# Two-layer hybrid gMLP and attention trunk: last gate tile's statistics deferred in layer 0, keys turned later, gated products' low parts moved to VectorE in layer 1

## The chip, the cores and the metric

The kernel runs on 1 core of one Trainium2 chip. The metric is the device time of one execution in microseconds; lower is better. Times below are medians of several executions, except where a profiled execution is named.

## What is computed

Two layers over 512 latent and 256 context tokens of width 1024, all in float32. In each layer one input projection gives queries (8 heads), keys and values (2 heads), and two 512-wide halves `u` and `g` of a gated mixer. The mixer normalises `gelu(g)` in groups of 128 channels, mixes it over 128 positions with a small matrix, and multiplies by `gelu(u)`:

```python
def chunk_gmlp(u, vg, w_s, b_s, g_norm):
    u = gelu(u)
    vg = group_layernorm(gelu(vg).reshape(b, n, 4, 128), g_norm)   # mean, variance of each group
    mixed = einsum('gpq,bnqgc->bnpgc', w_s, vg_by_chunks_of_128) + b_s
    return u * mixed
# one layer
attn = gqa(rope(rmsnorm(q)) * 64 ** -0.5, rope(rmsnorm(k)), v)     # context attends context, latents all
x = x + ga1 * (concat([attn, chunk_gmlp(u, g)]) @ w_out)
x = x + ga2 * (square(relu(modulate(rmsnorm(x), sh2, sc2) @ w_ff1)) @ w_ff2)
```

`sh`, `sc`, `ga` come from a modulation product of two condition vectors with `w_mod` (1024 x 6144 in each layer). In the last layer only the latents go past the keys and values.

## The kernel before, in words

**Numbers in two parts.** A float32 operand is split into a high part, rounded to the multiplier's format (`hi`, a cast by ScalarE), and the rest (`lo`, a subtraction by VectorE or GpSimd; `split`, L221 and L222). A product is three matmuls: high by high, high by low, low by high. Weights arrive as `raw` (two buffers), are split into a ring of five `hi`/`lo` pairs, and go back to the ring after their last use. The weights of layer 0's output projection are split by GpSimd (`PAR["WP"]`), the modulation weights of the later chunks are loaded straight into ring pairs and used in plain float32 (`mod_chunk`, L354).

**Order.** The program is written once, and a scheduler in the tile framework fixes each engine's order before the run. The author steers it with a virtual clock (`Flow`): each matmul advances it, and `fl.defer(delay, f)` has `f` written so much later. In the run every engine works through its own fixed list, one after the other.

**Layer 0, projections (about 55 to 168 us).** `sink_kv` and `sink_q` take the keys and queries of a pair of 128-token tiles (`tp` = 0, 1, 2; 2 is the context): norm and rotation (`qk`), then a split into a stack `k` (`stack`, one buffer, L722 to L725), then eight TensorE transposes and two copies (`turn`, L735, L736), `late(tp)` after the projection. After them come the `u` tiles and the gate tiles (`sink_g`, two column halves by three tile pairs). For a gate tile VectorE does the two steps of GELU (L802, L806), the statistics of four groups (L854, L855), a reciprocal square root of ten small instructions (L857, L301 to L311), and the normalisation (L860); ScalarE and GpSimd split the result (L221, L222); 13.6 us of virtual time later comes the mixing: twelve small matmuls into PSUM (`pt<-ws,e` and `pt<-ws,acc`, L217), scale and bias by VectorE (L884), product with `u` by GpSimd (L889).

**Layer 0, attention (from about 168 us).** Four context tiles of 128 queries of a head come first (`attn_tile`): scores into `pa`, maximum by VectorE (L982), exponential by ScalarE (L985), transposes by TensorE (L1001), split of the transposed weights (L1003, L1004), product with the values. Between them stand products that fill: modulation chunks (L354, with a transpose by VectorE, L362, and four small matmuls, L367) and the output projection of the gated products. `make_gm` prepares these products: it writes all mixings still due, then splits the four `U` tiles (L931 casts, L932 subtractions; the first two on VectorE, the other two on GpSimd).

**Layer 1** has the same stages with 512 tokens. GpSimd does its square roots (L298), the sums and products of the rotation (L707, L717), and the splits of the output weights. Its `make_gm` stands behind the last query tile, in front of attention, with low parts again two on VectorE and two on GpSimd.

PSUM holds two buffers each of `a` (scores, `u` tiles), `b` (projections, values, modulation) and `t` (transposes, mixings, small products): a product that needs a buffer waits until the last reader of the product two before it is done.

Of the kernel before, what the change touches and what calls it, by code (L numbers as in the profile page):

```python
# [8 lines left out]
F32 = mybir.dt.float32  # L9
F32R = mybir.dt.float32r  # L10
# [161 lines left out]
def trunk(ctx: ExitStack, tc: tile.TileContext, xT, pk1, pk2, rope, wsT, w_mod, w_tok, w_u, w_out, w_ff1, w_ff2, outT):  # L172
# [16 lines left out]
    def unit(tag, shape, dt=F32R):  # L189
        return units.tile(shape, dt, tag=tag, name=nm(tag))  # L190
# [10 lines left out]
    def te(dt=F32):  # L201
        return tmp.tile([128, 512], dt, tag="e", name=nm("e"), bufs=3)

    def small(n, dt=F32, tag="m", bufs=9):
        return tmp.tile([128, n], dt, tag=tag, name=nm(tag), bufs=bufs)
# [88 lines left out]
    def rsqrt(v, n, l=0):  # L294

        if l:
            y = small(n)
            pool_e.tensor_tensor(out=y, in0=v, in1=mhalf[:, 0:n], op=ALU.pow)  # L298
            return y
        yi = small(n, I32)  # L300
        vec.tensor_scalar(yi, v.bitcast(I32), -0.5, 1595932665.0, op0=ALU.mult, op1=ALU.add)  # L301
        y = yi.bitcast(F32)
        t, r = small(n), small(n)
        vec.tensor_tensor(out=t, in0=y, in1=y, op=ALU.mult)
        vec.scalar_tensor_tensor(out=t, in0=t, scalar=-0.703952253, in1=v, op0=ALU.mult, op1=ALU.mult)
        vec.scalar_tensor_tensor(out=y, in0=t, scalar=1.681914091, in1=y, op0=ALU.add, op1=ALU.mult)
        vec.tensor_tensor(out=t, in0=y, in1=y, op=ALU.mult)
        vec.tensor_tensor(out=r, in0=t, in1=v, op=ALU.mult)
        vec.tensor_scalar(t, r, 0.375, -1.25, op0=ALU.mult, op1=ALU.add)
        vec.tensor_tensor(out=t, in0=t, in1=r, op=ALU.mult)  # L310
        vec.scalar_tensor_tensor(out=y, in0=t, scalar=1.875, in1=y, op0=ALU.add, op1=ALU.mult)  # L311
        return y
# [364 lines left out]
    def layer(l, h, nxt, K, kv=None, kv0=0):  # L677
# [76 lines left out]
            fl.defer(PAR["QK%d" % l] if wait is None else wait, one)  # L754

        def late(tp):
            return 13000.0 + 8000.0 * tp if tp < 2 else 18000.0

        def sink_kv(tp, ps, pool=False):
            heads = lambda a: a.rearrange("p (h d) -> p h d", d=64)  # L760
# [11 lines left out]
                vec.tensor_tensor(out=vd[:, :, :, 64:128], in0=vps, in1=vd[:, :, :, 0:64].bitcast(F32), op=ALU.subtract)  # L772
            turned(t1, 2, 1, tp, [(kA, [(0, 0), (1, 0)]), (kB, [(0, 64), (1, 64)])], late(tp) if pool else None)

        def sink_q(grp):
            def f(tp, ps, pool=False):
                if tp == 0:
                    for f_ in mixes if grp and l else ():
                        f_()
                    Q.extend(unit(f"B{3 + grp * 2 + i}", [128, 2, T]) for i in range(2))  # L780
                ps = [p.rearrange("p (h d) -> p h d", d=64) for p in ps] if isinstance(ps, list) else ps.rearrange("p t (h d) -> p t h d", d=64)
                t1 = qk(ps, tp, 4, 0, pool)
                turned(t1, 4, 0, tp, [(Q[grp * 2 + i], [(2 * i, 0), (2 * i + 1, 0)]) for i in range(2)], late(tp) + 4000.0 if pool else None)
            return f
# [63 lines left out]
        def sink_g(gp):  # L848
            def f(tp, ps):
                v = gelu2(None, ps.rearrange("p t n -> p (t n)"), [128, 512])  # L850
                st = small(24, tag="bn", bufs=2).rearrange("p (a b) -> p a b", b=6)
                mv = small(8, tag="mv", bufs=2).rearrange("p (a b) -> p a b", b=2)
                for i in range(4):
                    vec.bn_stats(out=st[:, i, :], in_=v[:, i * 128:i * 128 + 128])  # L854
                    vec.bn_aggr(out=mv[:, i, :], in_=st[:, i, :])  # L855
                ve = small(4)
                vec.tensor_scalar(ve, mv[:, :, 1], 4 * EPS, None, op0=ALU.add)  # L857
                r = rsqrt(ve, 4, l)
                for i in range(4):
                    (pool_e if l in PAR['VG'] else vec).tensor_scalar(v[:, i * 128:i * 128 + 128], v[:, i * 128:i * 128 + 128], mv[:, i, 0:1], r[:, i:i + 1], op0=ALU.subtract, op1=ALU.mult)  # L860
                if len(mixes) > 1:
                    mixes[-2]()
                if l:
                    vg = unit(("B5", "B6")[len(mixes) % 2], [128, 2, 512])
                    vg = [vg[:, 0, :], vg[:, 1, :]]
                else:
                    vg = [te(F32R), tmp.tile([128, 512], F32R, tag="acc0", name=nm("acc0"), bufs=1) if len(mixes) % 2 else te(F32R)]
                split(*vg, v, pool_e if l in PAR['VL'] else vec)

                @once  # L870
                def mixing():
                    mx = pt((128, 2, 256))
                    for g in range(2):
                        for t in range(2):
                            c = slice(t * 256 + g * 128, t * 256 + g * 128 + 128)
                            w = slice((gp * 2 + g) * 128, (gp * 2 + g) * 128 + 128)
                            for i, (a, b) in enumerate(((0, 0), (0, 1), (1, 0))):
                                mm(mx[:, g, t * 128:t * 128 + 128], vg[a][:, c], ws[:, b, w], i == 0, i == 2, 128)
                    u = U[gp][:, :, tp * 256:tp * 256 + 256]
                    e = tsm([128, 2, 256])  # L880
                    for g in range(2):
                        G_ = gp * 2 + g
                        to = u if G_ == LATE[l] else e
                        vec.scalar_tensor_tensor(out=to[:, g, :].rearrange("p (t q) -> p t q", t=2), in0=mx[:, g, :].rearrange("p (t q) -> p t q", t=2),  # L884
                                                 scalar=gnh[:, G_:G_ + 1], in1=P2("bs")[:, G_ * 128:G_ * 128 + 128].unsqueeze(1).broadcast_to([128, 2, 128]),
                                                 op0=ALU.mult, op1=ALU.add)
                    gs = [g for g in range(2) if gp * 2 + g != LATE[l]]
                    gs = slice(gs[0], gs[-1] + 1)
                    pool_e.tensor_tensor(out=u[:, gs], in0=e[:, gs], in1=u[:, gs], op=ALU.mult)  # L889
                mixes.append(mixing)  # L890
                fl.defer(PAR["G%d" % l], mixing)
            return f

        with region('proj%d' % l):
# [22 lines left out]
        with region('q%d' % l):  # L917
            for g in range(2) if l else ():
                qp = TokProj(l, 1 + g, h, NP, sink_q(g))
                for tp in range(NP):  # L920
                    qp.bank(tp)

        GM = []

        def make_gm():
            for f in mixes:
                f()
            for g in range(4):
                gm = unit(f"A{g}", [128, 2, T])
                src = U[g // 2][:, g % 2, 0:TQ]  # L930
                act.copy(gm[:, 0, 0:TQ], src)  # L931
                (pool_e if g > 1 else vec).tensor_tensor(out=gm[:, 1, 0:TQ], in0=src, in1=gm[:, 0, 0:TQ].bitcast(F32), op=ALU.subtract)  # L932
                GM.append(gm)


        def gate(i, m, off, n, src):
            for a, b, cond in ((0, SEQ, 0), (SEQ, T, 1)):
# [113 lines left out]
                                fl.fill0(goal)  # L1051

        def gm_out():
            make_gm()
            yield from proj4(("out", l, 0), GM, 2, [dense], "b")

        def mods(js):
# [262 lines left out]
```

## Time and profile before

| | |
|---|---|
| median of 3 runs | 1504.56 us (1504.34 to 1506.78) |
| the profiled execution, its own time | 1504.58 us |
| its span, first to last instruction | 1502.8 us |
| TensorE busy | 1452.6 us (97%) |
| mean granted TensorE clock | 0.993 |
| TensorE busy in 100 to 200 us | 88.50 of 100 us |
| TensorE busy in 1000 to 1100 us | 97.24 of 100 us |

The profile shows for each instruction when it began and how long it took, and puts idle time of an engine down to the one that released it. A line of the chain or of the timeline gives start, duration, engine, source line, operation, output from inputs. "Idle before" stands in square brackets with the releaser behind the arrow. PE is TensorE, DVE VectorE, ACT ScalarE, POOL GpSimd, SP the queue that issues loads.

### The profile page before, as it was taken

What the parts mean: (1) busy time and instruction counts of PE and PEld (TensorE: products, weight loads), DVE (VectorE), ACT (ScalarE), POOL (GpSimd) and SP (SyncE); (2) the same over time, 40 slices, a digit from 0 to 9 for tenths busy, and PEclk for the clock granted to TensorE, in tenths of its full rate; (3) what the DMA queues carried; (4) which work ended last, traced back from release to release, by engine and by line L of the source; (5) the groups of instructions that cost most, each with busy time, mean ns of one, the idle gap of its engine ahead of it and who ended that gap; (6) DMA issues with size and microseconds to landing.
All of it is one profiled execution on the core that took longest, in us unless ns stands there. A gap on an engine that the chain in (4) does not pass through costs nothing.

```text
span 1502.8 us, 21987 instructions
## 1 busy us (share of the span) xinstructions
PE 1452.6 (97%) x8626; PEld 1276.0 (85%) x8626; DVE 893.1 (59%) x1603; ACT 638.0 (42%) x1081; POOL 359.9 (24%) x335
## 2 busy tenths in 40 slices
PE   6999799999999999999999999999999999999998
PEld 3889677798889899898989889897889888888887
DVE  5838867787755555444444536766887544444443
ACT  3542345665545453433333324536774333322221
POOL 0332331312045552322323213256122000000000
PEclk9999899999999999999999999999999999999999
DMA  9312524201134334333333311221001323333221
GB/s 365 106 57 86 181 89 171 94 15 43 61 111 129 116 120 127 104 122 112 127 113 126 99 56 52 90 85 57 29 1 57 113 98 98 98 99 98 99 97 58
DMA packets 50088, 148.78 MB, mean 99 GB/s; under 512 B 5440, under 2 KB 6976, under 8 KB 49984
## 3 DMA queue, kind: packets, MB, share of 16 engines
q1 hardware_dynamic: 49408, 146.72, 29.4%
q8 instruction: 68, 1.11, 0.3%
q10 hardware_dynamic: 576, 0.66, 0.1%
q14 instruction: 36, 0.29, 0.1%
HBM read 145.26 MB, written 2.10 MB: 98 GB/s over the span
## 4 chain that ended last, share of the span: by engine, by line
PE 83%; DVE 8%; ACT 3%; POOL 3%; issue 2%; DMA 1%; SPq 0%; POOLq 0%; ACTq 0%; DVEq 0%
PE pa L217 54%; PE pb L217 21%; PE pt L1001 3%; PE pt L217 2%; PE pb L354 2%; POOL m L298 1%; ACT hi L221 1%; DVE lo L222 1%; DMA A<-in_w_mod 1%; DVE X L941 1%; PE pt L735 1%; DVE B L1121 1%; POOL lo L222 1%; DVE s L860 0%; ACT w L985 0%
## 5 line engine op out<-in xcount | busy, mean ns | idle before, releaser
L217 PE MATMUL pa<-A,hi 128*128 128x384 f32 (+2 forms) x1728 | 458.6, 348 | 1.8 <-ACT w L1114 1.0
L221 ACT CAST hi<-raw 128x1024 fp32r<-128x1024 f32 x168 | 176.5, 1051 | 467.4 <-PE pa L217 386.0
L222 DVE TENSOR_TENSOR lo<-raw,hi 128x1024 fp32r<-128x1024 f32 x152 | 193.2, 1271 | 238.6 <-ACT hi L221 235.0
L217 PEld LDWEIGHTS pa<-A,hi 128*128 128x128 f32 x1728 | 310.8, 188 | 26.0 <-ACT w L1114 2.7
L217 PE MATMUL pa<-A,lo 128*128 128x384 f32 (+2 forms) x864 | 299.3, 347 | 0.0
L217 PE MATMUL pa<-B,hi 128*128 128x512 f32 (+1 forms) x900 | 239.8, 355 | 3.6 <-DVE X L941 3.6
L403 POOL TENSOR_TENSOR C<-C,s 128x512 f32<-128x512 f32 x112 | 164.4, 1483 | 315.8 <-ACT s L402 273.9
L217 PEld LDWEIGHTS pa<-B,hi 128*128 128x128 f32 x900 | 158.7, 188 | 31.7 <-DVE X L941 5.9
L217 PEld LDWEIGHTS pa<-A,lo 128*128 128x128 f32 x864 | 162.8, 189 | 10.6
L941 DVE SCALAR_TENSOR_TENSOR X<-pa,modT,X 128x512 f32<-128x512 f32 x126 | 82.9, 660 | 141.8 <-PE pa L217 141.8
L217 PE MATMUL pb<-B,hi 128*128 128x512 f32 (+1 forms) x600 | 156.7, 349 | 2.0 <-DVE X L941 2.0
L217 PE MATMUL pa<-B,lo 128*128 128x512 f32 (+1 forms) x450 | 157.7, 354 | 0.0
L941 DVE SCALAR_TENSOR_TENSOR X<-pb,modT,X 128x512 f32<-128x512 f32 (+3 forms) x116 | 70.9, 619 | 83.9 <-PE pb L217 83.6
L217 PE MATMUL pb<-hi,A 128*128 128x256 f32 (+1 forms) x608 | 118.3, 291 | 0.5 <-DVE m L715 0.5
L217 PEld LDWEIGHTS pb<-B,hi 128*128 128x128 f32 x600 | 104.2, 189 | 16.5 <-DVE X L941 3.2
L217 PE MATMUL pb<-B,lo 128*128 128x512 f32 (+1 forms) x300 | 104.6, 349 | 0.0
L217 PEld LDWEIGHTS pb<-hi,A 128*128 128x128 f32 x608 | 97.0, 191 | 2.2 <-PE pb L217 0.7
L217 PEld LDWEIGHTS pa<-B,lo 128*128 128x128 f32 x450 | 84.0, 188 | 11.3
L402 ACT ACTIVATE s<-k,silu 128x512 f32<-128x512 f32 x112 | 77.0, 716 | 38.4 <-DMA k<-in_w_mod 29.0
L217 PE MATMUL pb<-lo,A 128*128 128x256 f32 (+1 forms) x304 | 87.7, 288 | 0.0
L985 ACT ACTIVATE w<-pa,m 128x768 f32<-128x768 f32 (+1 forms) x80 | 65.6, 820 | 35.2 <-DVE m L982 33.4
L1004 DVE TENSOR_TENSOR A<-pt,A 128x384 fp32r<-128x384 f32 (+1 forms) x144 | 73.3, 536 | 11.1 <-ACT A L1003 9.3
(196 smaller groups left out, 2203.3 us busy)
## 6 DMA issues: line engine op xcount, KB each, us to landing
raw<-in_w_ff SPq DMA_DIRECT2D x128, 512.0 KB, 3.5
k<-in_w_mod SPq DMA_DIRECT2D x96, 256.0 KB, 3.1
raw<-in_w_tok SPq DMA_DIRECT2D x16, 512.0 KB, 3.5
raw<-in_w_out SPq DMA_DIRECT2D x16, 512.0 KB, 3.5
lo<-in_w_mod SPq DMA_DIRECT2D x16, 512.0 KB, 4.5
hi<-in_w_mod SPq DMA_DIRECT2D x16, 512.0 KB, 4.2
A<-in_w_mod SPq DMA_DIRECT2D x8, 512.0 KB, 9.9
B<-in_w_mod SPq DMA_DIRECT2D x8, 512.0 KB, 9.7
```

The costliest lines, as they stand in the source:

```text
L217: pe.matmul(out, a, b, start=start, stop=stop)
L221: act.copy(hi, src)
L222: (eng or vec).tensor_tensor(out=lo, in0=src, in1=hi.bitcast(F32), op=ALU.subtract)
L298: pool_e.tensor_tensor(out=y, in0=v, in1=mhalf[:, 0:n], op=ALU.pow)
L354: pe.matmul(ps[q:q + 32, :], S32[:, k, :], ws_[k2 // 2][:, k2 % 2 * 512:(k2 % 2 + 1) * 512], start=k < ns, stop=k >= KT - ns)
L402: act.activation(p, w, AF.Copy, scale=s)
L403: pool_e.tensor_tensor(out=a, in0=a, in1=p, op=ALU.add)
L735: pe.transpose(p[:, o:o + 128], stk[:, t, hh, c0:c0 + 128].bitcast(F32), ident)
L941: vec.scalar_tensor_tensor(out=xs, in0=src[:, s - off:e - off], scalar=modT[l][:, i * 8 + m, cond:cond + 1], in1=xs, op0=ALU.mult, op1=ALU ...
L985: act.activation(p, ps[:, 0:nk], AF.Exp, bias=nmx, accum_out=sm)
L1001: pe.transpose(tp_[:, (kt - k0) * 128:(kt - k0) * 128 + 128], p[:, kt * 128:kt * 128 + 128], ident)
L1004: vec.tensor_tensor(out=ptl[:, k0:k0 + step, d], in0=src, in1=pth[:, k0:k0 + step, d].bitcast(F32), op=ALU.subtract)
```

## The change

Three edits. First, in `sink_g` everything behind GELU (statistics, square root, normalisation, split) becomes a function `rest`; for the last gate tile of layer 0 (`n == 2 * NP - 1`) it is deferred by 8.0 us of virtual time, and its mixing by 21.6 instead of 13.6; all others run it at once as before. Second, `late` gives longer delays to tile pairs 1 and 2. Third, `make_gm` moves up in the code, is called in layer 1 from the last query tile's `sink_q` ahead of its norm, and has all four low parts on VectorE in layer 1.

```diff
         def late(tp):
-            return 13000.0 + 8000.0 * tp if tp < 2 else 18000.0
+            return 13000.0 + 11000.0 * tp if tp < 2 else 22000.0
...
+        def make_gm():
+            for f in mixes:
+                f()
+            for g in range(4):
...
+                act.copy(gm[:, 0, 0:TQ], src)
+                (pool_e if g > 1 and not last else vec).tensor_tensor(out=gm[:, 1, 0:TQ], in0=src, in1=gm[:, 0, 0:TQ].bitcast(F32), op=ALU.subtract)
...
         def sink_q(grp):
             def f(tp, ps, pool=False):
...
+                if last and grp and tp == NP - 1:
+                    for f_ in mixes:
+                        f_()
+                    make_gm()
                 t1 = qk(ps, tp, 4, 0, pool)
...
         def sink_g(gp):
             def f(tp, ps):
                 v = gelu2(None, ps.rearrange("p t n -> p (t n)"), [128, 512])
...
+                vg, n = [], len(mixes)
+
+                @once
+                def rest():
...
                 @once
                 def mixing():
+                    rest()
                     mx = pt((128, 2, 256))
...
                 mixes.append(mixing)
-                fl.defer(PAR["G%d" % l], mixing)
+                if l == 0 and n == 2 * NP - 1:
+                    fl.defer(8000.0, rest)
+                    fl.defer(8000.0 + PAR["G0"], mixing)
+                else:
+                    rest()
+                    fl.defer(PAR["G%d" % l], mixing)
...
         def gm_out():
-            make_gm()
+            if not GM:
+                make_gm()
```

What this does to the engines' lists is shown at three places. The rows are in the order in which an engine takes them; a name has the tile's buffer and number.

VectorE at the start of layer 0's attention, before. `mv_1854` is the last gate tile's statistics, `m_1863` to `m_1868` its square root, `pa_1902` the scores of the first attention tile:

```order
L857 TENSOR_SCALAR m_1863<-mv_1854 128x4
L301 TENSOR_SCALAR m_1865<-m_1863 128x4
L304 TENSOR_TENSOR m_1867<-m_1865 128x4
L305 SCALAR_TENSOR_TENSOR m_1867<-m_1867,m_1863 128x4
L306 SCALAR_TENSOR_TENSOR m_1865<-m_1867,m_1865 128x4
L307 TENSOR_TENSOR m_1867<-m_1865 128x4
L308 TENSOR_TENSOR m_1868<-m_1867,m_1863 128x4
L982 TENSOR_REDUCE m_1905<-pa_1902 128x1
L309 TENSOR_SCALAR m_1867<-m_1868 128x4
```

The same place after. `m_1769`, `m_1770` belong to the gate tile before the last one (`s_1750`), `s_1848` is the last one, `pa_1853` and `pa_1906` are the scores of the first two attention tiles, `s_1883` a mixing:

```order
L995 TENSOR_REDUCE m_1856<-pa_1853 128x1
L309 TENSOR_SCALAR m_1769<-m_1770 128x4
L818 SCALAR_TENSOR_TENSOR s_1848<-s_1848,pb_1787 128x512
L310 TENSOR_TENSOR m_1769<-m_1769,m_1770 128x4
L1000 RECIPROCAL m_1861<-m_1859 128x1
L311 SCALAR_TENSOR_TENSOR m_1767<-m_1769,m_1767 128x4
L880 TENSOR_SCALAR s_1750<-s_1750,mv_1756,m_1767 128x128 x4
L822 SCALAR_TENSOR_TENSOR s_1848<-s_1848,pb_1787 128x512
L874 BN_STATS bn_2018<-s_1848 128x6 x2
L905 SCALAR_TENSOR_TENSOR s_1883<-pt_1870,gnh_173,k_5_96 128x256 x2
L1017 TENSOR_TENSOR A_308_1888<-pt_1889,A_307_1887 128x2x128
L995 TENSOR_REDUCE m_1909<-pa_1906 128x1
```

The row in front of these is the other half of the same square root (L308). The first maximum has moved ahead of the last gate tile's GELU and of the end of the gate tile before it; the last tile's own square root stands 16 rows further down, behind the maximum of the fourth attention tile.

GpSimd from the split of the last gate tile but one to the last mixing's product, before. `lo_1959`, `lo_2016`, `lo_2080` are low parts of output weights, `acc_307_1899` the low part of the last gate tile:

```order
L222 TENSOR_TENSOR e_1784<-s_1750,e_1783 128x512
L889 TENSOR_TENSOR C_101_483<-s_1894,C_101_483 128x2x256
L222 TENSOR_TENSOR lo_1959<-raw_1956,hi_1958 128x1024
L222 TENSOR_TENSOR lo_2016<-raw_2013,hi_2015 128x1024
L990 COPY rc_1912<-m_1910 128x64
L990 COPY rc_1948<-m_1946 128x64
L222 TENSOR_TENSOR acc_307_1899<-s_1848,e_1898 128x512
L990 COPY rc_1912<-m_1975 128x64
L990 COPY rc_1948<-m_2004 128x64
L222 TENSOR_TENSOR lo_2080<-raw_2077,hi_2079 128x1024
```

And after, where `acc_359_2047` is the low part of the last gate tile:

```order
L910 TENSOR_TENSOR C_101_483<-s_1883,C_101_483 128x2x256
L222 TENSOR_TENSOR lo_1927<-raw_1924,hi_1926 128x1024
L1003 COPY rc_1916<-m_1914 128x64
L222 TENSOR_TENSOR lo_1960<-raw_1957,hi_1959 128x1024
L1003 COPY rc_1863<-m_1943 128x64
L1003 COPY rc_1916<-m_1978 128x64
L910 TENSOR_TENSOR C_101_483<-s_2000,C_101_483 128x2x256
L1003 COPY rc_2070<-m_2068 128x64
L222 TENSOR_TENSOR lo_2080<-raw_2077,hi_2079 128x1024
L222 TENSOR_TENSOR acc_359_2047<-s_1848,e_2046 128x512
```

The low part of the last gate tile has moved behind the third split of output weights. TensorE's list has the matching products in another order up to the last mixing, and the same list from there on.

VectorE in layer 1, at the gated products, before (`k_10054` is the stack of a query tile, `m_10107` the norm of the last one):

```order
L715 TENSOR_SCALAR m_10029<-m_10029 128x8
L723 TENSOR_TENSOR k_10054<-w_9917,k_10054 128x8x64
L932 TENSOR_TENSOR A_1693_10145<-C_1548_9139,A_1693_10145 128x512
L932 TENSOR_TENSOR A_1694_10148<-C_1548_9139,A_1694_10148 128x512
L698 TENSOR_REDUCE m_10107<-s_10105 128x8
```

And after:

```order
L723 TENSOR_TENSOR k_10054<-w_9917,k_10054 128x8x64
L784 TENSOR_TENSOR A_1680_10105<-C_1548_9139,A_1680_10105 128x512
L784 TENSOR_TENSOR A_1681_10108<-C_1548_9139,A_1681_10108 128x512
L784 TENSOR_TENSOR A_1682_10111<-C_1549_9140,A_1682_10111 128x512
L784 TENSOR_TENSOR A_1683_10114<-C_1549_9140,A_1683_10114 128x512
L698 TENSOR_REDUCE m_10119<-s_10117 128x8
```

Two subtractions came in; the two on GpSimd behind its L717 are gone from its list. The lists of TensorE and ScalarE in layer 1 have not changed.

More of the change, by code (lines that the diff above doesn't have):

```diff
@@ L773, in sink_kv @@
             turned(t1, 2, 1, tp, [(kA, [(0, 0), (1, 0)]), (kB, [(0, 64), (1, 64)])], late(tp) if pool else None)
+        GM = []
+        def make_gm():
+            for f in mixes:
+                f()
+            for g in range(4):
+                gm = unit(f"A{g}", [128, 2, T])
+                src = U[g // 2][:, g % 2, 0:TQ]
+                act.copy(gm[:, 0, 0:TQ], src)
+                (pool_e if g > 1 and not last else vec).tensor_tensor(out=gm[:, 1, 0:TQ], in0=src, in1=gm[:, 0, 0:TQ].bitcast(F32), op=ALU.subtract)
+                GM.append(gm)
         def sink_q(grp):
@@ L850, in f @@
                 v = gelu2(None, ps.rearrange("p t n -> p (t n)"), [128, 512])
[L851 to L867, printed above, removed]
@@ L868, in f @@
-                split(*vg, v, pool_e if l in PAR['VL'] else vec)
+                vg, n = [], len(mixes)
+                @once
+                def rest():
+                    st = small(24, tag="bn", bufs=2).rearrange("p (a b) -> p a b", b=6)
+                    mv = small(8, tag="mv", bufs=2).rearrange("p (a b) -> p a b", b=2)
+                    for i in range(4):
+                        vec.bn_stats(out=st[:, i, :], in_=v[:, i * 128:i * 128 + 128])
+                        vec.bn_aggr(out=mv[:, i, :], in_=st[:, i, :])
+                    ve = small(4)
+                    vec.tensor_scalar(ve, mv[:, :, 1], 4 * EPS, None, op0=ALU.add)
+                    r = rsqrt(ve, 4, l)
+                    for i in range(4):
+                        (pool_e if l in PAR['VG'] else vec).tensor_scalar(v[:, i * 128:i * 128 + 128], v[:, i * 128:i * 128 + 128], mv[:, i, 0:1], r[:, i:i + 1], op0=ALU.subtract, op1=ALU.mult)
+                    if n > 1:
+                        mixes[n - 2]()
+                    if l:
+                        two = unit(("B5", "B6")[n % 2], [128, 2, 512])
+                        vg.extend((two[:, 0, :], two[:, 1, :]))
+                    else:
+                        vg.extend((te(F32R), tmp.tile([128, 512], F32R, tag="acc0", name=nm("acc0"), bufs=1) if n % 2 else te(F32R)))
+                    split(*vg, v, pool_e if l in PAR['VL'] else vec)
@@ L890, in f @@
                 mixes.append(mixing)
-                fl.defer(PAR["G%d" % l], mixing)
+                if l == 0 and n == 2 * NP - 1:
+                    fl.defer(8000.0, rest)
+                    fl.defer(8000.0 + PAR["G0"], mixing)
+                else:
+                    rest()
+                    fl.defer(PAR["G%d" % l], mixing)
             return f
@@ L921, in layer @@
                     qp.bank(tp)
[L923 to L933, printed above, removed]
         def gate(i, m, off, n, src):
```

## The prediction

> **What bounds the kernel now.** I read the page first, then who waited for whom on TensorE, then the engines' timelines at the waits that the change touches.
>
> ```profile
> span 1502.8 us, 21987 instructions
> PE 1452.6 (97%) x8626; PEld 1276.0 (85%) x8626; DVE 893.1 (59%) x1603; ACT 638.0 (42%) x1081; POOL 359.9 (24%) x335
> ```
>
> TensorE is busy for all but 1502.8 - 1452.6 = 50.2 us. A change that removes no product can gain only from these, and from time in which the granted clock was low. The waits of TensorE, longest first in total:
>
> ```profile
> PE pb L354 <- DMA A<-in_w_mod: 12.4, 1, 12.4
> PE pt L1001 <- ACT w L985: 8.5, 3, 7.5
> PE pb L217 <- POOL A L932: 4.2, 4, 2.1
> ...
> PE pt L735 <- POOL k L723: 2.2, 1, 2.2
> PE pb L354 <- issue: 2.1, 1, 2.1
> ```
>
> The 12.4 us are the first load. The three edits stand at the next four rows: the first transposes of layer 0's attention wait 7.5 us for an exponential, the 2.1 us of "issue" lie just ahead of that, low parts of the gated products cost 4.2, and a key or query stack 2.2.
>
> The wait of 7.5 us is not ScalarE's. VectorE at this place, then GpSimd, then TensorE:
>
> ```profile
> 171.61 0.16 DVE L308 TENSOR_TENSOR m<-m,m 128x4 f32<-128x4 f32 x1
> ...
> 173.90 0.68 DVE L806 SCALAR_TENSOR_TENSOR s<-s,pb 128x512 f32<-128x512 f32 x1
> ...
> 177.75 2.26 DVE L301 TENSOR_SCALAR m<-m 128x4 int32<-128x4 int32 x1
> 180.04 2.25 DVE L304 TENSOR_TENSOR m<-m 128x4 f32<-128x4 f32 x1
> 182.33 0.16 DVE L305 SCALAR_TENSOR_TENSOR m<-m,m 128x4 f32<-128x4 f32 x1
> ...
> 183.00 0.42 DVE L982 TENSOR_REDUCE m<-pa 128x1 f32<-128x256 f32 x1
> ```
>
> ```profile
> 177.64 4.64 POOL L222 TENSOR_TENSOR lo<-raw,hi 128x1024 fp32r<-128x1024 f32 x2
> ```
>
> ```profile
> 171.08 0.51 PE L217 MATMUL pa<-B,B 128*128 128x256 f32 x2
> ...
> 184.07 0.69 PE L1001 MATMUL pt<-c,w 128*128 128x128 f32 x2 [7.46 <-ACT w L985]
> ```
>
> The maximum of the first scores (L982), which the exponential needs, stands in VectorE's list behind the last gate tile's square root. Two instructions of it on 128x4 elements take 2.26 and 2.25 us where the next takes 0.16: they end at 180.01 and 182.29, and GpSimd's two splits of output weights run from 177.64 to 182.28. Each had to wait for one GpSimd instruction to end. The Trainium skill ("SBUF — State Buffer", section "Who interferes with whom") says that VectorE and GpSimd share a port pair and that the later of two that need it fully blocks; by that rule, too, the statistics and not the maximum are caught, and the trace agrees with 2.26 against 0.16 us.
>
> The idle time costs a second time. TensorE's busy time and granted clock (the last number but two) in the stretch from the end of the gate projection to the last mixing, and in some windows of 3.41 us in which the clock changed or might have:
>
> ```profile
> 168.42:179.83 11.41, 6.09 (x50) 2.64 (x48) 11.10 (x35) 4.66 (x7) 4.70 (x3) 1.00 0.93 331
> 179.83:190.07 10.24, 5.50 (x22) 2.93 (x22) 7.46 (x24) 2.91 (x9) 4.37 (x6) 0.50 0.41 142
> 190.07:199.30 9.23, 8.73 (x72) 6.09 (x71) 6.13 (x18) 5.45 (x16) 4.26 (x5) 1.00 0.33 99
> ```
>
> ```profile
> 80.85:84.26 3.41, 1.43 (x10) 1.43 (x11) 1.95 (x6) 1.67 (x6) 3.33 (x4) 1.00 0.02 5
> 84.26:87.67 3.41, 3.41 (x14) 3.23 (x12) 0.95 (x3) 1.78 (x5) 3.33 (x4) 0.50 0.00 0
> ...
> 173.00:176.42 3.42, 1.73 (x16) 0.50 (x16) 3.42 (x16) 2.44 (x4) 1.29 (x1) 1.00 0.99 390
> ...
> 183.24:186.66 3.42, 2.09 (x15) 1.45 (x15) 2.84 (x13) 1.65 (x6) 0.24 (x1) 0.50 0.47 153
> ```
>
> After a window with 1.43 us of work the clock fell to 0.50, after one with 1.73 it did not; at 0.50, a window with 2.09 us did not bring it back. At full clock the stretch holds 6.09 + 5.50 / 2 + 8.73 = 17.57 us of TensorE work, and it takes 11.41 + 10.24 + 9.23 = 30.88.
>
> **The change part by part. Keys turned later (edit 2): nothing.** The stack that TensorE waits 2.2 us for is the first tile pair's, whose delay has not changed; its place in every list is the same. GpSimd still reaches it late:
>
> ```profile
> 81.51 1.26 POOL L723 TENSOR_TENSOR k<-e,k 128x512 fp32r<-128x512 f32 x1
> ```
>
> It ends at 82.77, and TensorE resumes at 82.83 in before. The turn that does move (the third pair's query) falls among 84 to 168 us, where TensorE is covered by projections. Bounds: no gain and no loss beyond half a microsecond, since the turns need no more work.
>
> **Statistics deferred (edit 1).** Durations for what follows, from the groups of 168 to 200 us:
>
> ```profile
> L222 POOL TENSOR_TENSOR lo<-raw,hi 128x1024 fp32r<-128x1024 f32 x3 | 7.0, 2354 | 1.3 <-ACT hi L221 1.3
> L982 DVE TENSOR_REDUCE m<-pa 128x1 f32<-128x256 f32 x7 | 2.9, 414 | 0.0
> L884 DVE SCALAR_TENSOR_TENSOR s<-pt,gnh,k 128x256 f32<-128x256 f32 x6 | 2.7, 472 | 0.5 <-PE pt L217 0.5
> L1004 DVE TENSOR_TENSOR A<-pt,A 128x256 fp32r<-128x256 f32 x6 | 2.5, 424 | 1.3 <-ACT A L1003 1.2
> L889 POOL TENSOR_TENSOR C<-s,C 128x512 f32<-128x512 f32 x2 | 2.5, 1268 | 0.4 <-DVE mv L855 0.4
> L860 DVE TENSOR_SCALAR s<-s,mv,m 128x128 f32<-128x128 f32 x8 | 2.2, 342 | 0.0
> L222 POOL TENSOR_TENSOR acc<-s,e 128x512 fp32r<-128x512 f32 x1 | 1.3, 1267 | 0.4 <-ACT e L221 0.4
> ```
>
> What goes: the 7.46 and the 2.1 us, and the half clock. What is late next, from TensorE's new list:
>
> (a) First exponential. The maximum now follows L308, so it ends at 171.77 + 0.45 = 172.2; in before TensorE began 184.07 - 183.42 = 0.65 us behind the maximum's end, so 172.85. TensorE's work ahead of it (scores, four modulation products, one mixing) is what before did from 168.42 to 171.08. New wait 1.75 us.
>
> (b) Second exponential. Between the two maxima VectorE has two GELU steps (0.68 each), four L860 (1.1), two BN (0.5), two L884 (0.9), one L1004 and half a microsecond of small ones: 4.8 us, so the second maximum ends at 177.4 at most and TensorE resumes at about 177.8. TensorE has 3.6 us of products from 172.85. New wait 1.3.
>
> (c) The last tile's square root has not left GpSimd's reach, it has moved: GpSimd's second split of weights now runs until about 182.7, and VectorE comes to the root at 182.2. The 0.5 us lost are small, but behind the root stand the maximum, two L860 and the two L884 that free a `t` buffer; they end at about 186.4, while TensorE needs that buffer at 184.75. New wait 1.7.
>
> (d) The low part of the last gate tile stands behind the third split of weights (2.35) on GpSimd: product with `u` until 187.7, copy until 188.7, split until 191.1, low part until 192.4. TensorE is at the last mixing at 190.6. New wait 1.85.
>
> (e) Short waits for PSUM buffers that VectorE frees an instruction late: 0.2, 1.0 and 0.55 us, 1.75 together.
>
> The sum of (a) to (e) is 8.35. The stretch becomes 17.57 + 8.35 = 25.9 us against 30.88: **5.0 us gained.** Bounds: with (a) alone 30.88 - 19.3 = 11.6; with five microseconds more of waits, nothing. I take 5.0, because each of these waits is an instruction whose row exists. Behind the last mixing the lists are the same, and the two waits of about a microsecond for GpSimd's low parts in layer 0 stay.
>
> **Low parts in layer 1 (edit 3).** TensorE, VectorE and GpSimd there:
>
> ```profile
> 1021.50 0.39 PE L217 MATMUL pb<-A,hi 128*128 128x512 f32 x1
> 1024.03 0.50 PE L217 MATMUL pb<-A,hi 128*128 128x512 f32 x1 [2.14 <-POOL A L932]
> ...
> 1025.27 0.50 PE L217 MATMUL pb<-A,hi 128*128 128x512 f32 x1 [0.28 <-POOL A L932]
> ```
>
> ```profile
> 1018.35 2.38 DVE L932 TENSOR_TENSOR A<-C,A 128x512 fp32r<-128x512 f32 x2
> ```
>
> ```profile
> 1017.75 1.82 POOL L707 TENSOR_TENSOR w<-w,s 128x512 f32<-128x512 f32 x1
> 1019.53 2.10 POOL L298 TENSOR_TENSOR m<-m,mhalf 128x8 f32<-128x8 f32 x1
> ```
>
> VectorE's pair ends at 1020.73, having waited for L707 to end at 1019.57; the second of the pair ran within the time of L298. Two more at about 0.68 each end at 1021.4 and 1022.1; TensorE needs them at 1021.89 and 1022.6. Both waits go: 2.14 + 0.28 = 2.4. VectorE is 1.4 us later for the last query tile, whose PSUM buffer then comes free at about 1023.95, when TensorE asks for it; I take off 0.3. **2.1 us gained**, bounds 0 and 2.4.
>
> The Trainium skill's rule (same page and section) that the loser blocks for the whole instruction would hold three of the four subtractions until L298 ends at 1021.63. By it the third ends at 1023.7 and the gain is 0.6; the row of the pair speaks against it for L298.
>
> Total: 5.0 + 2.1 = 7.1. The profiled execution took 1504.58 us, 1.8 more than its span and next to the median of 1504.56, so 1504.58 - 7.1 = 1497.5.
>
> **The rivals.** R1, fewer new waits: if VectorE and GpSimd are a little earlier, (c) and (d) vanish, 3.55 more: 1493.9. For it, half of their lists there are short waits for others; against it, each is in one fixed list.
>
> R2, the clock: waits of 1.3 to 1.85 us leave 1.55 to 2.1 us of work in 3.41, near the 1.43 at which it fell. Two windows at 0.50 cost 2 x 1.7 = 3.4: 1500.9. The Trainium skill ("TensorE: Matmul & The Clock Gate", "Part 1: The HAM clock gate") lets the clock fall after an idle window; the trace had it fall after one that was 42% busy, so I go by the row.
>
> R3, the port in layer 1: GpSimd's L298 and L717 each get in between VectorE's subtractions and TensorE still waits 1.8: 5.0 + 0.6 gained, 1499.0.
>
> R4, the wait only moves: GpSimd reaches the last low part five microseconds later than in (d), because the third block of output weights, loaded behind modulation blocks, comes late. Layer 0 gains nothing: 1502.5. Against it, such a load takes 3.5 us:
>
> ```profile
> raw<-in_w_out SPq DMA_DIRECT2D x16, 512.0 KB, 3.5
> ```
>
> R5, slower: the clock falls at (a) and stays at 0.50 until the last mixing. Of 17.57 us of work 14.8 are left at 173.0; at half clock 29.6, to 202.6, and with (d) and some short waits 205. That is 5.7 later than 199.3; less 2.1 in layer 1, 1508.2. It decides if no window of the stretch is busy throughout; against it, a slow TensorE fills its windows, as in 84.26 to 87.67.
>
> **How the numbers follow.** Forecast 0.42, R1 0.18, R2 0.15, R3 0.10, R4 0.09, R5 0.06. About 0.2% (3.0 us) is what a measurement of this kernel tells from no change, so faster means under 1501.5: forecast, R1, R3 and two thirds of R2, 0.80. Same: R4 and the rest of R2, 0.14. Slower: R5, 0.06. The range goes from 1493.5 (R1) to 1501.5 (most of R2), leaving out R4, R5 and the edges.
>
> **What would show it.** Right: the first transposes of attention wait about 1.75 us and the clock stays at 1.00 from 168 to 194; the four subtractions of layer 1 stand on VectorE and no wait of 2 us follows; the wait of 2.2 us near 82 is there again. Wrong: a wait of over 3 us on the last mixing's low part, a new stretch at 0.50, or a third place at which TensorE loses what it won.

## The result and the profile after

| | before | after |
|---|---|---|
| median of 6 runs | 1504.45 us (1502.87 to 1506.78) | 1496.60 us (1495.60 to 1496.94) |
| the profiled execution, its own time | 1504.58 us | 1496.73 us |
| its span | 1502.8 us | 1494.9 us |
| TensorE idle in the span | 50.2 us | 39.8 us |

The ratio is 0.9945, with a 95% interval of 0.9932 to 0.9958: 7.85 us faster, where 7.1 were forecast. The waits of TensorE after the change, from the same view as in the prediction:

```profile
PE pb L354 <- DMA A<-in_w_mod: 12.0, 1, 12.0
...
PE pt L735 <- POOL k L723: 2.7, 2, 2.2
PE pt L1014 <- ACT w L998: 2.1, 2, 1.5
...
PE pt L217 <- POOL acc L222: 1.6, 1, 1.6
...
PE pb L217 <- POOL A L784: 0.3, 1, 0.3
```

The wait of transposes for an exponential (now L1014 for L998) has fallen from 8.5 to 2.1 us, and the one for GpSimd's low parts of the gated products (now L784) from 4.2 to 0.3. The 2.1 us of "issue" are gone. New are 1.6 us for the last gate tile's low part. The wait for a stack near 82 us is still 2.2, as forecast, with 0.4 more for the next stack.

Where the time came from is read from one instruction that both kernels have. The tenth exponential of layer 0's attention, before and after:

```profile
211.19 0.47 ACT L985 ACTIVATE w<-pa,m 128x256 f32<-128x256 f32 x1 [2.46 <-DVE m L982]
```

```profile
205.36 0.47 ACT L998 ACTIVATE w<-pa,m 128x256 f32<-128x256 f32 x1 [2.56 <-DVE m L995]
```

So 5.83 us are won by then; 0.34 of these stood already at the end of the gate projection, in front of the attention (168.08 us against 168.42). The rest of the 7.9 us of span, about 2.0, is won in layer 1. In layer 1, VectorE and GpSimd after the change:

```profile
1012.54 3.58 DVE L784 TENSOR_TENSOR A<-C,A 128x512 fp32r<-128x512 f32 x4
```

```profile
1011.95 1.81 POOL L707 TENSOR_TENSOR w<-w,s 128x512 f32<-128x512 f32 x1
1013.72 2.10 POOL L298 TENSOR_TENSOR m<-m,mhalf 128x8 f32<-128x8 f32 x1
```

All four subtractions end at 1016.12, and TensorE then has only two short waits in place of 2.14 and 0.28 us: 0.23 for the last query tile's buffer, which was forecast at 0.3, and 0.22 for an exponential.

The start of layer 0's attention: TensorE's waits from 168 us on, and the rows of GpSimd that end the last of them:

```profile
172.43 0.44 PE L1014 MATMUL pt<-c,w 128*128 128x128 f32 x2 [1.47 <-ACT w L998]
177.07 0.44 PE L1014 MATMUL pt<-c,w 128*128 128x128 f32 x2 [0.64 <-ACT w L998]
180.03 1.05 PE L354 MATMUL pb<-hi,S 128*32 128x512 f32 x2 [0.15 <-DVE s L362]
191.21 0.33 PE L217 MATMUL pt<-ws,acc 128*128 128x128 f32 x1 [1.56 <-POOL acc L222]
```

```profile
187.54 2.38 POOL L222 TENSOR_TENSOR lo<-raw,hi 128x1024 fp32r<-128x1024 f32 x1
189.89 1.26 POOL L222 TENSOR_TENSOR acc<-s,e 128x512 fp32r<-128x512 f32 x1
```

The chain of step (d) is there as forecast: third split, low part, mixing. From the end of the gate projection to the end of the last mixing, and the window of the clock with the wait of 1.56 us and the two behind it (TensorE's busy time stands behind the length, its granted clock is the last number but two):

```profile
168.08:193.07 24.99, 21.11 (x143) 11.78 (x142) 20.64 (x78) 12.95 (x32) 13.55 (x14) 0.97 0.73 273
```

```profile
188.41:191.83 3.42, 1.86 (x14) 1.69 (x14) 2.45 (x8) 1.86 (x7) 3.30 (x4) 1.00 0.91 346
191.83:195.24 3.41, 3.41 (x23) 2.95 (x22) 2.00 (x4) 0.00 (x0) 1.17 (x1) 0.50 0.27 109
195.24:198.65 3.41, 3.41 (x13) 3.13 (x13) 1.36 (x5) 2.77 (x6) 2.10 (x3) 0.50 0.32 96
```

The stretch takes 24.99 us against 30.88: 5.89 won. Idle time fell from 30.88 - 20.32 = 10.56 us to 24.99 - 21.11 = 3.88, so 6.7 are won in waits and 0.8 given back in busy time. Behind the wait of 1.56 us the clock was 0.50 for two windows, which stood among the rivals and not in the forecast; a new stretch at 0.50 was one of the prediction's own signs of being wrong. The two waits for GpSimd's low parts in layer 0, which were to stay, went with it: 1.08 and 0.70 us in before, at 204.59 and 206.43 us, and one of 0.35 now. Behind the last mixing 0.4 us are given back, so that layer 0's attention gave about 5.5.

### The profile page after: what moved, and what is told of

Read it like the earlier page. It is cut to its first block, busy times and chain, and to the rows that moved or that the text cites. A ratio compares the mean times of both kernels' runs of the same rounds, so it can differ in the third digit from the quotient of the medians.

```text
span 1494.9 us, 21987 instructions
## 1 busy us (share of the span) xinstructions
PE 1455.1 (97%) x8626; PEld 1277.7 (85%) x8626; DVE 891.0 (60%) x1605; ACT 638.1 (43%) x1081; POOL 356.2 (24%) x333
## 4 chain that ended last, share of the span: by engine, by line
PE 82%; DVE 9%; ACT 3%; POOL 2%; issue 2%; DMA 1%; SPq 0%; POOLq 0%; ACTq 0%; DVEq 0%
PE pa L217 54%; PE pb L217 20%; PE pt L1014 3%; PE pt L217 2%; PE pb L354 2%; DVE lo L222 1%; POOL m L298 1%; ACT hi L221 1%; DVE s L880 1%; DVE X L954 1%; DMA A<-in_w_mod 1%; DVE B L1135 1%; POOL lo L222 1%; PE pt L735 0%; DVE m L995 0%
## 5 line engine op out<-in xcount | busy, mean ns | idle before, releaser
L998 ACT ACTIVATE w<-pa,m 128x768 f32<-128x768 f32 (+1 forms) x80 | 65.6, 820 | 31.5 <-DVE m L995 27.4
```

The source lines that it names most:

```text
L998: act.activation(p, ps[:, 0:nk], AF.Exp, bias=nmx, accum_out=sm)
```

## The experiments

Theory: the three edits act in separate places. Layer 0's gain is the first maximum's place ahead of a square root that GpSimd's splits hold. What stays is bound by chains behind VectorE and GpSimd. The rivals stand with each run. Times are medians; "before" was run beside each group (1504.31 to 1504.86 us).

**Each edit alone.** The first run has the changed kernel's `sink_g` and the other two edits undone:

```diff
-            return 13000.0 + 11000.0 * tp if tp < 2 else 22000.0
+            return 13000.0 + 8000.0 * tp if tp < 2 else 18000.0
...
-                if last and grp and tp == NP - 1:
-                    for f_ in mixes:
-                        f_()
-                    make_gm()
...
-                (pool_e if g > 1 and not last else vec).tensor_tensor(...)
+                (pool_e if g > 1 else vec).tensor_tensor(...)
```

> Only the deferred statistics of the last gate tile; turns and layer 1 as in the kernel before. Theory (the three edits act in separate places and add up; the layer 0 gain of 5.8 us is the statistics' own): 1504.5 - 5.8 = 1498.7 us, between 1497.7 and 1499.7; waits of TensorE of 1 to 2 us on the first exponential and on the last gate tile's low part, two windows of 3.41 us at clock 0.50 behind the latter, and in layer 1 the waits of 2.1 and 0.3 us for GpSimd's low parts as before. Rival (the later turns are part of the layer 0 gain, because TensorE, with the turns where they were, reaches attention later or meets a stack that is not ready): under 5.0 us gained, 1499.5 us or more.

Measured: 1497.62 us, ratio 0.9950 (0.9937 to 0.9964). The waits are 1.4 and 1.5 us, as the theory has it; of its two windows at 0.50 behind the latter there was one, and there was one at 172.72 us, behind the first wait. The gain of 6.95 is a little over the theory's edge of 6.8. The profiled execution, the slowest of the five (1500.09 us, with another window at 0.50 near 1019 us), has the tenth exponential at 204.97 us, 6.2 ahead of before. So the rival falls: layer 0's gain is there without the later turns.

The second run is the kernel before with the new line of `late` only:

```diff
-            return 13000.0 + 8000.0 * tp if tp < 2 else 18000.0
+            return 13000.0 + 11000.0 * tp if tp < 2 else 22000.0
```

> Only the longer delays of the turns. Theory (the turns need no more work and TensorE is covered by projections): within 0.5 us of the kernel before, and the wait of 2.2 us for the first pair's stack and its window at clock 0.50 are there as before. Rival (the later turns take away a wait at the gate projection, which was 0.33 us further ahead after the change): 0.5 to 1.0 us faster with a wait on the rotation's square root missing near 146 us. The other rival is a loss of up to 1 us where a turn meets a stack that GpSimd has not finished (0.42 us near 88 us after the change).

Measured: 1504.05 us beside 1504.57, ratio 0.9996 (0.9987 to 1.0005). No difference that the runs can tell, as forecast; the rival's 0.5 us is not excluded. The wait of 0.54 us for a rotation's square root near 147 us, which before and the other runs with the old delays have, is gone. The wait of 2.2 us is there, without its window at 0.50. A stack near 87 us is waited for, but the later turns are not shown to cause that: the next run, with the old delays and no window at 0.50 there either, has the same wait. This run's rows, then that run's:

```profile
81.56 0.66 PE L735 MATMUL pt<-c,k 128*128 128x128 f32 x4 [2.24 <-POOL k L723]
86.62 1.09 PE L735 MATMUL pt<-c,k 128*128 128x128 f32 x8 [1.40 <-POOL k L723]
```

```profile
87.37 1.09 PE L735 MATMUL pt<-c,k 128*128 128x128 f32 x8 [1.48 <-POOL k L723]
```

The third run is the changed kernel with the other two edits undone:

```diff
-            return 13000.0 + 11000.0 * tp if tp < 2 else 22000.0
+            return 13000.0 + 8000.0 * tp if tp < 2 else 18000.0
...
-                if l == 0 and n == 2 * NP - 1:
+                if False:
```

> Only the four low parts on VectorE in layer 1; layer 0 as before. Theory: 2.0 us faster, 1502.5 us, between 1501.9 and 1503.1; the four subtractions take about 3.6 us from their first start, the first held by one GpSimd instruction and the others inside GpSimd's square root; no wait over 0.5 us for a low part. Rival (each subtraction is held by a whole GpSimd instruction): the four take 5 us or more and under 1.0 us is gained.

Measured: 1502.60 us, ratio 0.9984 (0.9975 to 0.9993), 2.0 us faster. The theory holds. The rival, a hold by each GpSimd instruction, would have left less than half of it. By the medians the three gains sum to 9.4 us against 7.85 for the change; each is uncertain by 1.3 to 2 us, so the runs can't tell whether they add up. In the profiles the runs with one edit each win 6.2 us by the tenth exponential and 2.0 in layer 1, the change 5.8 and 2.0.

**What the deferral wins: the hold by GpSimd, or the order.** The kernel before, with GpSimd's splits of layer 0's output weights cut from 1024 columns to 128 (in a single line; ScalarE fills the other 896 columns with the high parts, so that part of the product is left out; the order of the root and the first maximum is unchanged):

```diff
-                split(hi, lo, raw, pool_e if "%s%d" % key[:2] in PAR["WP"] else vec)
+                [act.copy(hi, raw), pool_e.tensor_tensor(out=lo[:, 0:128], in0=raw[:, 0:128], in1=hi[:, 0:128].bitcast(F32), op=ALU.subtract), act.copy(lo[:, 128:1024], raw[:, 128:1024])] if key[:2] == ('out', 0) else split(...)
```

> The kernel before, with GpSimd taking the low parts of layer 0's output weights for 128 of 1024 columns only, and ScalarE filling the other 896 columns with the high parts in place of the low ones (that part of the product is left out); the order of the square root and the first maximum on VectorE is as before. Theory (the root's two long instructions are held by GpSimd's splits, so the place behind the root is costly only because of these): they take 0.16 us each, the wait of 7.46 us falls by 4.2 to about 3.3 us, 1500.3 us, between 1499.0 and 1501.5, so that over half of what the deferral gained is GpSimd's hold and the rest is the order. Rival (the two instructions wait for something else, or the maximum has to wait for the scores): they stay above 1 us each, and the time is within 1 us of the kernel before.

Measured: 1499.51 us, ratio 0.9974 (0.9963 to 0.9986). VectorE at the root, GpSimd, and TensorE's next two waits:

```profile
175.73 0.38 DVE L301 TENSOR_SCALAR m<-m 128x4 int32<-128x4 int32 x1
176.14 0.37 DVE L304 TENSOR_TENSOR m<-m 128x4 f32<-128x4 f32 x1
176.55 0.16 DVE L305 SCALAR_TENSOR_TENSOR m<-m,m 128x4 f32<-128x4 f32 x1
```

```profile
175.63 0.86 POOL L272 TENSOR_TENSOR lo<-raw,hi 128x128 fp32r<-128x128 f32 x2
```

```profile
178.29 0.44 PE L1001 MATMUL pt<-c,w 128*128 128x128 f32 x2 [3.69 <-ACT w L985]
181.01 0.69 PE L1001 MATMUL pt<-c,w 128*128 128x128 f32 x2 [1.99 <-ACT w L985]
```

The two instructions follow the length of GpSimd's: 0.38 and 0.37 us beside splits of 0.43, where they took 2.26 and 2.25 beside splits of 2.3. That they wait for GpSimd is shown. The long wait falls from 7.46 to 3.69, near the 3.3 expected. But 1.99 us come back at the second exponential, and the 2.1 us ahead of it stay. TensorE's waits here are then 7.8 us, against 10.56 before and 3.88 after the change: of the 6.7 won in waits, 2.8 go with the hold alone. The share of the hold is not settled by that. In this run's list the second maximum stands behind four normalisations, and ahead of them in before's:

```profile
178.60 1.18 DVE L860 TENSOR_SCALAR s<-s,mv,m 128x128 f32<-128x128 f32 x4
179.71 0.41 DVE L982 TENSOR_REDUCE m<-pa 128x1 f32<-128x256 f32 x1
```

So part of the 1.99 us is this run's own order. By the first wait alone the hold is 3.8 of the 6.7; this run puts it between 2.8 and 3.8, and "over half" stays open. (The whole time also has shorter splits at later places, and is not the price of this stretch.)

**The deferral, shorter and longer.** The changed kernel with 4000.0 in both places, then with 12000.0:

```diff
-                    fl.defer(8000.0, rest)
-                    fl.defer(8000.0 + PAR["G0"], mixing)
+                    fl.defer(4000.0, rest)
+                    fl.defer(4000.0 + PAR["G0"], mixing)
```

> The changed kernel with the statistics deferred by 4.0 us of virtual time in place of 8.0 (mixing by 17.6). The first two maxima keep their places ahead of the square root, the low part of the last gate tile stands ahead of the third split of output weights, and the root stands where GpSimd makes its first two splits. Theory (GpSimd's splits hold the root's instructions, and with them every maximum behind): two of the root's instructions take over 1 us again, the third exponential comes 3 to 5 us late, a new wait of 2 to 4 us against the 1.56 saved; 1498.5 us, between 1497.0 and 1500.5. Rival (what counts is only that the first maximum is ahead of the root): 1496 us or less, since the wait on the low part goes.

Measured, with 4000.0: 1498.48 us, ratio 0.9953 (0.9936 to 0.9969), 1.9 slower than with 8000.0 by the medians. The intervals overlap, but the profiles agree: at the same instructions this kernel is 1.2 us ahead of the changed one from 92 to 167 us and 2.3 to 2.5 behind it from the tenth exponential on. VectorE's root, now inside GpSimd's splits, and TensorE's wait:

```profile
176.52 1.68 DVE L877 TENSOR_SCALAR m<-mv 128x4 f32<-128x4 f32 x1
...
178.44 2.23 DVE L304 TENSOR_TENSOR m<-m 128x4 f32<-128x4 f32 x1
```

```profile
175.81 2.37 POOL L222 TENSOR_TENSOR lo<-raw,hi 128x1024 fp32r<-128x1024 f32 x1
...
178.30 2.35 POOL L222 TENSOR_TENSOR lo<-raw,hi 128x1024 fp32r<-128x1024 f32 x1
```

```profile
181.75 1.92 PE L354 MATMUL pb<-hi,S 128*32 128x512 f32 x2 [2.95 <-DVE m L307]
```

Two of the root's instructions are held again, and TensorE waits 2.95 us for what stands behind the root, though the first maximum is ahead of it. The rival falls: where the root stands relative to the splits counts as well as the first maximum.

> The changed kernel with the statistics deferred by 12.0 us in place of 8.0 (mixing by 25.6); TensorE's last mixing moves behind two more attention products and a block of the output projection. Theory (behind the last mixing layer 0 is bound by the chain product, cast, low part, which now begins about 4 us later with nothing to fill it): 2 to 4 us lost, 1499.5 us, between 1498.0 and 1501.0, with the waits for GpSimd's low parts of the gated products over 1 us each. Rival (TensorE fills the time with attention): within 1 us of the changed kernel, 1495.6 to 1497.6 us.

Measured, with 12000.0: 1498.20 us, ratio 0.9952 (0.9937 to 0.9967), 1.6 slower than with 8000.0 by the medians, inside the theory's bounds and below its middle. In the profiles it is 2.6 us ahead of the changed kernel from 92 to 167 us, 0.9 behind at 207 and 0.2 to 0.5 behind from 221 on, so about 2.9 us are lost between. The waits are those of the chain behind the last mixing, cast and low part:

```profile
197.54 0.62 PE L217 MATMUL pb<-A,hi 128*128 128x384 f32 x2 [1.44 <-ACT A L783]
199.44 0.69 PE L217 MATMUL pb<-A,hi 128*128 128x384 f32 x1 [1.27 <-POOL A L784]
```

**The new wait (d) and the clock behind it.** The changed kernel with the low part of the last gate tile on VectorE:

```diff
-                    split(*vg, v, pool_e if l in PAR['VL'] else vec)
+                    split(*vg, v, pool_e if l in PAR['VL'] and not (l == 0 and n == 2 * NP - 1) else vec)
```

> The changed kernel with the low part of the last gate tile of layer 0 on VectorE in place of GpSimd, so that it no longer stands behind the third split of output weights. Theory (the wait of 1.56 us empties the window in front of 191.8 us and so costs two windows at clock 0.50, 3.4 us, besides itself): the wait goes, the clock stays at 1.00 from 168 to 200 us, 1496.6 - 5.0 = 1491.6 us, between 1491.0 and 1493.0. Rival A (the clock falls there anyway, because of the short products around it): only the wait goes, 1495.0 us. Rival B (VectorE, busy throughout, takes the low part late and with it every exponential behind it): no gain, 1496 us or more.

Measured: 1495.02 us, ratio 0.9933 (0.9920 to 0.9945). The time is that of rival A, but the rival is wrong and so is the theory's sum. The clock did stay at 1.00, and the wait of 1.56 is gone, yet others came in its place (the last row is the tenth exponential):

```profile
189.47 0.44 PE L217 MATMUL pt<-ws,e 128*128 128x128 f32 x2 [1.21 <-DVE A L1017]
...
196.72 0.44 PE L217 MATMUL pb<-A,hi 128*128 128x384 f32 x1 [1.27 <-POOL A L784]
198.50 0.44 PE L217 MATMUL pb<-A,hi 128*128 128x384 f32 x1 [0.62 <-POOL A L784]
...
203.50 0.47 ACT L998 ACTIVATE w<-pa,m 128x256 f32<-128x256 f32 x1 [2.54 <-DVE m L995]
```

Not all of the 1.6 us is the edit's. At the end of the gate projection, in front of the edited place, this profiled execution is already 1.38 us ahead of the changed kernel's (166.70 us against 168.08), and at the tenth exponential 1.86 (203.50 against 205.36). So the edit won about 0.5 us. TensorE at half clock had cost little in the changed kernel: behind the last mixing it would have waited for GpSimd's low parts anyway. This run bought one wait and uncovered three. The next kernel takes those low parts to VectorE too:

```diff
-                (pool_e if g > 1 and not last else vec).tensor_tensor(...)
+                vec.tensor_tensor(...)
```

> As the version with the last gate tile's low part on VectorE, and the last two low parts of the gated products of layer 0 on VectorE as well, in place of GpSimd, where they took 1.81 us each behind the last mixing. Theory (behind the last mixing layer 0 is bound by the chain mixing, scale, product, cast, low part, so that what was won ahead of it came back as waits of 1.27 and 0.62 us for GpSimd's low parts): 0.95 us each on VectorE, 1.5 to 2 us less, 1493.3 us, between 1492.5 and 1494.2. Rival (VectorE is busy there with sums and maxima, and takes the low parts no earlier): 1494.5 us or more, with the wait named for VectorE.

Measured: 1493.88 us, ratio 0.9929 (0.9914 to 0.9943). The wait of 1.27 is 0.38 now and names VectorE, the one of 0.62 is gone; 1.1 us are won over the run before it by the medians, within the theory's bounds, though the two intervals overlap. Between the same instructions at 167 and 205 us the two profiles differ by 1.75 us, inside the theory's 1.5 to 2.

**The wait near 82 us, which the change left.** The changed kernel with the first pair's stacks on VectorE, with `tp` handed to `stack`:

```diff
-            (pool_e if l in PAR['SK'] else vec).tensor_tensor(out=stk[...], ...)
+            (pool_e if l in PAR['SK'] and not (l == 0 and tp == 0) else vec).tensor_tensor(out=stk[...], ...)
```

> The changed kernel with the low parts of the first tile pair's stacks of layer 0 on VectorE in place of GpSimd. Theory (the wait of 2.2 us near 82 us, which the change left, is GpSimd's full list of rotations, and the window at clock 0.50 behind it follows from the wait): 2.2 us, and 1.0 to 1.7 us more in executions that had the window: 1493.5 us, between 1492.7 and 1494.8. Rival (the next stack, the second pair's, already late by 0.4 to 1.4 us, takes the place of the first): under 1.0 us gained, 1495.6 us or more.

Measured: 1493.99 us, ratio 0.9931 (0.9916 to 0.9945). The number is the theory's and the trace is the rival's:

```profile
80.66 0.63 PE L735 MATMUL pt<-c,k 128*128 128x128 f32 x4 [0.75 <-DVE k L723]
85.95 1.09 PE L735 MATMUL pt<-c,k 128*128 128x128 f32 x8 [1.97 <-POOL k L723]
```

The waits sum to 2.7 us as in the changed kernel; the wait moved to the second pair. What is missing in the profiled execution is the window at clock 0.50 near 82 us. That is not shown to be the edit's doing: the run of the turns alone and the one with the last gate tile's low part on VectorE lacked it too, with the wait of 2.2 us in place. Those two gained 0.5 us on the changed kernel's profile between 80 and 95 us; this one gained 1.4 there, and another 0.9 had come ahead of 80 us, in front of the edit. So about 0.9 of the 2.6 us is shown to be the edit's, which is what the rival said.

All three moves together, and then with the second pair's stacks on VectorE too (`tp < 2` in place of `tp == 0`):

> The two before this one together: low parts of the last gate tile, of the gated products of layer 0 and of the first pair's stacks on VectorE. Theory: the gains add, 1493.3 - 3.1 = 1490.2 us, between 1489.4 and 1492.0, with the clock at 1.00 from 80 us on. Rival (one of the two gives nothing): 1493 us or more.

Measured: 1492.14 us, ratio 0.9920 (0.9905 to 0.9935), short of the theory by 1.9. One row says why: the wait for the second pair's stack is now 2.48. A window at 0.50 stands there too, from 85.75 us, where the theory had 1.00.

```profile
86.20 1.97 PE L735 MATMUL pt<-c,k 128*128 128x128 f32 x8 [2.48 <-POOL k L723]
```

> As the version with all three groups of low parts on VectorE, and the second tile pair's stacks on VectorE too, since the wait had moved to them (2.48 us near 86 us). VectorE was busy for only 1.4 of 6.8 us behind 84 us. Theory (the wait is GpSimd's list, whichever stack stands last in it): the 2.48 us go, 0.3 to 0.8 us of short waits stay, 1492.1 - 2.0 = 1490.1 us, between 1489.3 and 1491.3. Rival (the rotation ahead of the stacks, on GpSimd too, is what is late): the wait stays over 1.5 us, 1491.5 us or more.

Measured: 1488.78 us (1487.87 to 1488.99), ratio 0.9888 (0.9873 to 0.9903): 16.1 us under the 1504.86 of before, and an interval clear of the change's. No turn waits for GpSimd's stacks any more. This version beats both kernels and is faster than the theory's bounds: 3.4 us under the last version, where 2.0 were forecast. That wait is 2.48 of them; in the two profiles 3.9 us lie between 80 and 95 us, where the window at 0.50 behind the wait has gone too.

## Why the prediction was right, step by step

**Edit 2, nothing:** right as far as the runs can tell, also run by itself. The wait of 2.2 us stayed.

**Edit 3, 2.1 us:** right, 2.0 measured by itself and in the trace. The first subtraction was held until L707 ended, the other three had ended 0.3 us after L298's 2.10. By the rule of the Trainium skill that was weighed there ("SBUF — State Buffer", "Who interferes with whom"), 0.6 us would have been won; the run doesn't bear that out for L298.

**Edit 1, 5.0 us:** right in size, 5.5 in the trace, but that is luck: its two terms were off by 3.5 and 4.5 us, in opposite directions. The first term, 17.57 us of TensorE work at full clock, was too small, and taking it over from before was the step that failed. The stretch was busy for 21.11 us after the change. With the low part on VectorE and the clock at 1.00 throughout it was 20.71:

```profile
166.70:190.90 24.20, 20.71 (x144) 11.25 (x142) 21.99 (x76) 12.54 (x32) 12.02 (x12) 1.00 0.74 271
```

The prediction took the work to be the same in any order. The modulation products (L354) show that it is not. They alone, with the same 48 records, in before and after:

```profile
168.42:199.30 30.88, 8.10 (x48) 1.30 (x48) 0.83 0.58 199
```

```profile
168.08:193.07 24.99, 9.27 (x48) 1.45 (x48) 0.97 0.73 273
```

In before 1.92 of the 8.10 us lay at clock 0.50, so by the prediction's halving they are 7.1 us of work; after the change they are 9.27, all at full clock. Eight of these records next to each other take 1.05 us together. Where the list puts other products behind the first two, these two take as long, and the six that come later again 1.05. Before has one such pair (the 1.92 us, at half clock); after the change there are three, the one at 180.03 us shown above and these:

```profile
175.41 1.02 PE L354 MATMUL pb<-hi,S 128*32 128x512 f32 x2
...
184.52 1.04 PE L354 MATMUL pb<-hi,S 128*32 128x512 f32 x2
```

Two more pairs are 2.1 of the 3.1 us by which 20.71 exceeds 17.57. The rest is not traced; halving is a little too much for short products, since a pair of transposes takes 0.69 us at 0.50 and 0.44 at full clock. So "the idle time costs a second time" is not refuted (a pair alone took 1.92 us at 0.50 and 1.02 at full clock), but what the full clock saved the new order took back, and the net gain came from idle time. The second term, 8.35 us of new waits, was too large: 3.88. By its parts:

- (a) first exponential 1.47, forecast 1.75, and (d) last low part 1.56, forecast 1.85: the chains were right, each instruction in the place of the list that was said, (d) about 1 us earlier.
- (b) second exponential 0.64, forecast 1.3: VectorE ended the second maximum at 176.42, not 177.4 ("at most" had been taken as the value), and TensorE had 4.0 us of products ahead of it, not 3.6.
- (c) was forecast at 1.7 and is not there. VectorE came to the root earlier and lost only 0.3 us to GpSimd's second split, so that the fourth maximum began at 183.14:

```profile
181.47 0.49 DVE L877 TENSOR_SCALAR m<-mv 128x4 f32<-128x4 f32 x1
...
183.14 0.42 DVE L995 TENSOR_REDUCE m<-pa 128x1 f32<-128x256 f32 x1
```

- (e) short waits 0.15, forecast 1.75.

**The rivals.** R1 (fewer new waits) came true for (c), not for (d). R2 (two windows at 0.50) came true in the profile, but not its price of 3.4 us: those windows lay ahead of the gated products, where TensorE would have waited for GpSimd. The run with the low part on VectorE shows it: the wait gone and the clock back at 1.00 gave about 0.5 us together. R3, R4 and R5 did not occur.

## What to carry to other kernels

Where several short instructions stand ahead of the one that feeds the bottleneck engine, look at what a neighbour engine runs at that moment as well as at the order: here the hold alone was worth 2.8 to 3.8 of the 6.7 us of waits and the order the rest, and a deferral that put the root back inside the hold brought a wait of 2.95 us back. A wait that is removed uncovers the next chain: price a fix by the wait that will then end last, as the version at 1488.78 us, with three chains moved and then the one that they uncovered, shows against each alone. A new order can change the work as well as the waits: compare the busy time of the same products before and after. A stretch of half clock is little to win if its work ends at a wait anyway. And where two kernels differ by a microsecond, compare their profiles in front of the edit first.

## What the runs showed of the hardware

The windows in which the clock is granted don't start with the program. In the profile of before they begin at 84.26 us and every 3.413 us from there, in that of after at 82.59. So executions of one kernel differ in how many windows they lose: of before, one took 1506.36 us at a mean clock of 0.991 and another 1502.94 at 0.996. The same wait of 2.2 us near 82 us had a window at 0.50 behind it in the profiles of before and after and none in that of the turns alone. The Trainium skill ("TensorE: Matmul & The Clock Gate", "Part 1: The HAM clock gate") says that the window is free-running, and the traces agree. Its other statement, that the clock falls after an idle window, does not fit, and nor does the prediction's reading by busy time. In before:

```profile
15.99:19.41 3.42, 2.38 (x22) 1.27 (x20) 0.88 (x2) 1.04 (x1) 0.87 (x1) 1.00 1.04 416
19.41:22.82 3.41, 2.66 (x12) 0.92 (x12) 2.19 (x5) 0.72 (x1) 0.15 (x1) 0.50 1.02 406
...
203.73:207.14 3.41, 1.85 (x9) 1.53 (x10) 2.86 (x7) 1.24 (x5) 3.03 (x3) 1.00 0.01 2
207.14:210.55 3.41, 3.41 (x23) 3.29 (x22) 2.38 (x7) 1.59 (x5) 0.24 (x1) 1.00 0.23 77
```

It fell after a window with 2.38 us of busy time and not after one with 1.85, and in after it stayed at 0.50 behind a window that was busy throughout. What the gate counts stays open.

Not every instruction of VectorE is held. After the change a maximum and a subtraction ran at their usual length inside GpSimd's splits of 177.07 to 179.44 and 179.57 to 181.94 us:

```profile
177.51 0.41 DVE L995 TENSOR_REDUCE m<-pa 128x1 f32<-128x256 f32 x1
...
179.90 0.39 DVE L1017 TENSOR_TENSOR A<-pt,A 128x256 fp32r<-128x256 f32 x1
```

Each reads at most one input from SBUF; the other, `pa` or `pt`, is in PSUM. The Trainium skill ("SBUF — State Buffer", "Who interferes with whom") says that such instructions don't contend, outside the modes that use two ports, and the rows agree.
